# Where the high parts of the output projections' rows begin: from 160 to 288 modulo 512 bytes

## The chip, the cores and the metric

The kernel runs on one core of a Trainium2 chip. The metric is the device time of one execution in microseconds. Matmuls run on TensorE (PE), with weight loads shown as a row of their own (PEld); VectorE (DVE) and ScalarE (ACT) prepare operands; SyncE (SP) issues nearly all transfers.

## The reference

One layer of a transformer, 256 tokens of width 2048, all in float32. It is three blocks, each with an adaptive layer norm ahead and a gated residual with a second layer norm behind:

```python
h = _swiglu(_modulate(x, sh1, sc1), ffn1_w_in, ffn1_w_out)
x = _layernorm(ALPHA * x + 0.5 * (1 + g1) * h, ln1_g, ln1_b)
h = _token_mixer(_modulate(x, sh2, sc2), w_in, ..., w_out)
x = _layernorm(ALPHA * x + (1 + g2) * h, ln2_g, ln2_b)
h = _swiglu(_modulate(x, sh3, sc3), ffn2_w_in, ffn2_w_out)
x = _layernorm(ALPHA * x + 0.5 * (1 + g3) * h, ln3_g, ln3_b)
```

`_swiglu` is `(silu(gate) * up) @ w_out` with an inner width of 5632. The three products with `ffn1_w_out` (5632 x 2048), `w_out` (2048 x 2048) and `ffn2_w_out` (5632 x 2048) are the output projections of the title.

## The kernel before

Every float32 product is made of three products in the `fp32r` type. An operand is split in a high part (a cast on ACT, line 142) and a low part (what the cast lost, a subtraction on DVE, line 143), and `mm3` issues high x high (line 373), high x low (line 374) and low x high (line 375) into one accumulation. Three such matmuls are called a trio below.

In an output projection (`out_proj`) the rows, that is the activations, are the stationary operand (128 x 128, loaded on PEld), and the weights are the moving operand (128 x 512, streamed past them). For each k of 128 rows of the weights, each half `a` of the tokens and each block `b` of 512 columns there is one trio:

| line | moving operand | stationary operand |
|---|---|---|
| 373 | high part of weights (`hi`) | high part of rows (`hh`) |
| 374 | low part of weights (`lo`) | high part of rows (`hh`) |
| 375 | high part of weights (`hi`) | low part of rows (`hl`) |

The names in the trace are `o_f<-hi_f1o,hh` for the first feed-forward block (`f1o`), `f2o` for the second, and `o_mx<-hi_mxo,yhi` for the mixer, where the rows of the eight attention heads are `yhi`, `ylo`, and those of the other eight k are `yh`, `yl`, tiles of another pool that nothing here moves. In the feed-forward blocks `h_rows` splits the rows, two k at a time, into one of six buffers `hh` and one of six `hl`; the very first two k of each block go to two tiles of their own, laid out elsewhere, that the trace calls `h`.

Where a tile begins in a partition's memory follows from the order in which a pool's tiles are asked for. All weight buffers are whole multiples of 512 bytes long, and so are `hh`, `hl`, `yhi`, `ylo` and the activations `xhi`, `xlo` of the other products, so each kind has one place modulo 512:

| operand | modulo 512 before |
|---|---|
| `hi`, high parts of all weights | 288 |
| `lo`, low parts of all weights | 160 |
| `hh`, `hl`, `yhi`, `ylo` | 160 |
| `h` (both parts) | 448 |
| `xhi`, `xlo` | 480 |
| `yh`, `yl` | 8 places each, 128 to 392 |

`gap` asks for a tile that nothing uses, to move what comes after it:

```python
    for t in ("hhi", "hlo"):
        lnp.tile([P, 2, T], F32R, tag=t, bufs=6, name=f"{t}_place")
    gap(lnp, 320, "gap_h")
```

Ahead of the projections and between them, form A products (`s`, `gu_f`, `fs`, `fh`, `pr_f`) have the weights stationary and 256 tokens moving, and products such as `gf` have `xhi`, `xlo` stationary and 512 columns of weights moving, like an output projection with other rows.

Of the kernel before, what the change touches and what calls it, by code (L numbers as in the profile page):

```python
# [8 lines left out]
F32R = mybir.dt.float32r  # L9
# [6 lines left out]
P = 128  # L16
T = 256
# [6 lines left out]
NFH = 8  # L24
# [10 lines left out]
def layer_kernel(  # L35
# [13 lines left out]

    def gap(pool, nbytes, name):  # L50
        pool.tile([P, nbytes // 4], F32, tag=name, name=name)

    wp.tile([P, 4, 520], F32, tag="raw", bufs=3, name="raw_place")
    gap(wp, 320, "gap_hi")
    wp.tile([P, 1024], F32R, tag="hi", bufs=6, name="hi_place")
    wp.tile([P, 10], F32, tag="sums", bufs=4, name="sums_place")
# [179 lines left out]
    def need(n):  # L238
        while parts_done[0] < n and next(ada_left["g"], 0) != 0:
            owed[0] = 0  # L240
# [234 lines left out]
    def ln_params(g, b, tag):  # L475
        lg = lnp.tile([P, D], F32, tag="lg", name=f"lg_{tag}")
        lb = lnp.tile([P, D], F32, tag="lb", name=f"lb_{tag}")
        SP.dma_start(lg, g.to_broadcast([P, D]))
        SP.dma_start(lb, b.to_broadcast([P, D]))
        return lg, lb  # L480
# [308 lines left out]
    xp.release()  # L789
    lnp = tc.alloc_tile_pool(name="ln1", bufs=1, **right)  # L790
    lgb = ln_params(ln1_g, ln1_b, "1")
    for t in ("hhi", "hlo"):
        lnp.tile([P, 2, T], F32R, tag=t, bufs=6, name=f"{t}_place")
    gap(lnp, 320, "gap_h")
    need(1)
    W = w_in[0]

# [12 lines left out]
    def finish1(products, add_up, st):  # L810
        need(2)
        hp.release()
        ent["xp"] = tc.alloc_tile_pool(name="xp2", bufs=1)
        gap(ent["xp"], 544, "gap_x")
        ent["np"] = tc.alloc_tile_pool(name="np2", bufs=1)
        ent["f"] = (products, add_up, st)
# [358 lines left out]
    lnp = tc.alloc_tile_pool(name="ln2", bufs=1)  # L1175
# [5 lines left out]
            need(4)  # L1181

    gap(lnp, 224, "gap_y")
    yhi, ylo = (lnp.tile([P, NFH, T], F32R, name=f"y{i}") for i in ("hi", "lo"))


    def y_rows(k):
# [67 lines left out]
    for j in range(2, 10):  # L1255
# [8 lines left out]
        for f in range(2):  # L1264
            i = 2 * j + f
# [11 lines left out]
    for j in range(2, 10):  # L1277
# [7 lines left out]
        for f in range(2):  # L1285
            i = 2 * j + f
# [9 lines left out]
    xp.release()  # L1296
    lnp = tc.alloc_tile_pool(name="ln3", bufs=1, **right)
    lgb = ln_params(ln3_g, ln3_b, "3")
    for t in ("hhi", "hlo"):
        lnp.tile([P, 2, T], F32R, tag=t, bufs=6, name=f"{t}_place")  # L1300
    gap(lnp, 320, "gap_h")

    def finish3(products, add_up, st):
        to_out(products, add_up, st, lgb)
# [33 lines left out]
```

## Time and profile before

| | us |
|---|---|
| median of 3 runs | 1966.28 (1964.45 to 1966.31) |
| profiled execution | 1965.57 |
| its span, first to last instruction | 1963.8 |
| around the span | 1.8 |
| PE busy | 1896.5 |
| DVE busy | 1495.8 |
| first feed-forward output projection, in the span | 541.3 to 786.0 |
| mixer's output projection | 1109.4 to 1206.0 |
| second feed-forward output projection | 1709.1 to 1952.0 |

Mean granted clock of TensorE is 0.993. A matmul's duration in the trace runs from its start to its modelled end and overlaps the next one's; what a matmul costs in a stream without gaps is the distance from its start to the next start, called its pitch below.

### The profile page before, as it was taken

How to read it: one execution, taken by the hardware profiler on the slowest of the kernel's cores; microseconds unless marked ns; L12 is line 12 of the kernel's file. 1: busy time of each engine (PE TensorE's matmuls, PEld its weight loads, DVE VectorE, ACT ScalarE, POOL GpSimd, SP SyncE). 2: the span in 40 equal slices, each digit the busy share in tenths (PEclk: the TensorE clock that was granted, in tenths of full speed). 3: DMA queues.
4: the chain of work that ended last, by engine and by line, in shares of the span. 5: the costliest groups of instructions: out<-in, count | busy, mean ns of one | idle time of the engine just before them, and what ended most of it. 6: DMA issues, size and time to landing. Idle time of an engine off the chain costs nothing.

```text
span 1963.8 us, 32259 instructions
## 1 busy us (share of the span) xinstructions
PE 1896.5 (97%) x13057; PEld 1727.6 (88%) x13057; DVE 1495.8 (76%) x1878; ACT 961.1 (49%) x1396; POOL 6.3 (0%) x17
## 2 busy tenths in 40 slices
PE   3999999999999999899999998999999999999997
PEld 3999999999988888588999786899999999988885
DVE  7788889777788897678888688777766655555776
ACT  3644354443454554745755544555444444444553
POOL 0000000000000000000000000000000000000000
PEclk9999999999999999999999999999999999999999
DMA  9998978899898786489888784888777765655552
GB/s 331 342 315 278 314 253 289 290 305 326 281 343 303 268 303 208 140 292 319 270 300 278 273 285 151 285 292 274 241 248 249 261 216 190 236 193 193 193 193 86
DMA packets 301820, 510.89 MB, mean 260 GB/s; under 512 B 10818, under 2 KB 158690, under 8 KB 300648
## 3 DMA queue, kind: packets, MB, share of 16 engines
q1 hardware_dynamic: 300808, 505.70, 76.2%
q0 software_dynamic: 864, 3.15, 0.5%
q8 instruction: 102, 1.67, 0.4%
q14 instruction: 46, 0.38, 0.0%
HBM read 506.71 MB, written 2.10 MB: 259 GB/s over the span
## 4 chain that ended last, share of the span: by engine, by line
PE 83%; DVE 8%; DMA 5%; ACT 2%; issue 2%; SPq 0%; DVEq 0%; ACTq 0%
PE gu_f L374 8%; PE gu_f L375 8%; PE gu_f L373 8%; PE o_f L373 8%; PE o_f L375 8%; PE o_f L374 8%; PE s L373 3%; PE s L375 3%; PE s L374 3%; DMA raw_s<-in_ffn_w_in_dram 2%; DVE lo_s L143 2%; PE fs L375 1%; PE fs L374 1%; PE fs L373 1%; PE o_mx L373 1%
## 5 line engine op out<-in xcount | busy, mean ns | idle before, releaser
L157 DVE SCALAR_TENSOR_TENSOR acc<-ar,csil,acc 128x1024 f32<-128x1024 f32 x242 | 307.8, 1272 | 74.6 <-DMA ar<-in_w_ada_dram 72.9
L373 PE MATMUL s<-xhi_f,hi_s 128*128 128x256 f32 x768 | 215.0, 280 | 3.0 <-ACT hi_s L142 3.0
L375 PE MATMUL s<-xhi_f,lo_s 128*128 128x256 f32 x768 | 214.4, 280 | 1.9 <-DVE lo_s L143 1.9
L374 PE MATMUL s<-xlo_f,hi_s 128*128 128x256 f32 x768 | 214.2, 279 | 0.0
L375 PE MATMUL gu_f<-xhi_f,lo_f2i 128*128 128x256 f32 x768 | 212.0, 276 | 0.0
L373 PE MATMUL gu_f<-xhi_f,hi_f2i 128*128 128x256 f32 x768 | 212.0, 276 | 0.0
L374 PE MATMUL gu_f<-xlo_f,hi_f2i 128*128 128x256 f32 x768 | 212.0, 276 | 0.0
L143 DVE TENSOR_TENSOR lo_f2i<-raw_f2i,hi_f2i 128x1024 fp32r<-128x1024 f32 x96 | 117.6, 1225 | 91.4 <-ACT hi_f2i L142 91.4
L373 PE MATMUL gu_f<-xhi_f,hi_f1i 128*128 128x256 f32 x640 | 176.8, 276 | 0.0
L375 PE MATMUL gu_f<-xhi_f,lo_f1i 128*128 128x256 f32 x640 | 176.7, 276 | 0.0
L374 PE MATMUL gu_f<-xlo_f,hi_f1i 128*128 128x256 f32 x640 | 176.7, 276 | 0.0
L142 ACT CAST hi_f2i<-raw_f2i 128x1024 fp32r<-128x1024 f32 x96 | 100.8, 1050 | 135.4 <-PE gu_f L374 124.6
L373 PEld LDWEIGHTS s<-xhi_f,hi_s 128*128 128x128 f32 x768 | 146.2, 190 | 3.5 <-ACT hi_s L142 3.4
L142 ACT CAST hi_s<-raw_s 128x1024 fp32r<-128x1024 f32 x96 | 96.6, 1049 | 107.0 <-DMA raw_s<-in_ffn_w_in_dram 85.9
L375 PEld LDWEIGHTS s<-xhi_f,lo_s 128*128 128x128 f32 x768 | 145.9, 190 | 2.9 <-DVE lo_s L143 2.8
L374 PEld LDWEIGHTS s<-xlo_f,hi_s 128*128 128x128 f32 x768 | 146.4, 191 | 0.0
L374 PEld LDWEIGHTS gu_f<-xlo_f,hi_f2i 128*128 128x128 f32 x768 | 144.2, 188 | 0.2
L373 PEld LDWEIGHTS gu_f<-xhi_f,hi_f2i 128*128 128x128 f32 x768 | 144.2, 188 | 0.2
L375 PEld LDWEIGHTS gu_f<-xhi_f,lo_f2i 128*128 128x128 f32 x768 | 144.2, 188 | 0.0
L142 ACT CAST hh<-hT 128x512 fp32r<-128x512 f32 x130 | 80.0, 622 | 127.9 <-PE o_f L374 126.6
L143 DVE TENSOR_TENSOR lo_f2o<-raw_f2o,hi_f2o 128x1024 fp32r<-128x1024 f32 x88 | 107.7, 1224 | 44.9 <-ACT hi_f2o L142 44.8
L143 DVE TENSOR_TENSOR lo_s<-raw_s,hi_s 128x1024 fp32r<-128x1024 f32 x96 | 114.5, 1221 | 30.6 <-ACT hi_s L142 30.6
(452 smaller groups left out, 5385.2 us busy)
## 6 DMA issues: line engine op xcount, KB each, us to landing
ar<-in_w_ada_dram SPq DMA_DIRECT2D x288, 512.0 KB, 5.4
raw_s<-in_ffn_w_in_dram SPq DMA_DIRECT2D x48, 1024.0 KB, 6.1
raw_f2i<-in_ffn_w_in_dram SPq DMA_DIRECT2D x48, 1024.0 KB, 5.2
raw_f1o<-in_ffn_w_out_dram SPq DMA_DIRECT2D x44, 1024.0 KB, 7.4
raw_f2o<-in_ffn_w_out_dram SPq DMA_DIRECT2D x44, 1024.0 KB, 5.1
raw_f1i<-in_ffn_w_in_dram SPq DMA_DIRECT2D x40, 1024.0 KB, 7.7
raw_mxo<-in_w_out_dram SPq DMA_DIRECT2D x16, 1024.0 KB, 6.1
raw_fh<-in_ffn_w_in_dram SPq DMA_DIRECT2D x16, 1024.0 KB, 7.3
```

The costliest lines, as they stand in the source:

```text
L142: S.copy(hi, src)
L143: return V.tensor_tensor(out=lo, in0=src, in1=hi.bitcast(F32), op=ALU.subtract)
L157: V.scalar_tensor_tensor(out=acc, in0=raw, scalar=csil[:, k:k + 1], in1=acc, op0=ALU.mult, op1=ALU.add)
L373: PE.matmul(o, ah, bh, start=start, stop=False)
L374: PE.matmul(o, ah, bl, start=False, stop=False)
L375: PE.matmul(o, al, bh, start=False, stop=stop)
```

## The change

In the pool of the first and of the third layer norm the low parts of the rows are placed first (still 160 modulo 512), then 128 bytes that nothing uses, then the high parts (now 288), then 192 bytes. In the second, `ylo` comes first (160), then 128 bytes, then `yhi` (288). No other tile changes its place modulo 512; `hl` and `ylo` change their absolute place, in the same memory. The order of instructions on each of the five engines, their shapes and the waits they carry are the same in both programs, row for row.

```diff
-    for t in ("hhi", "hlo"):
+    for t in ("hlo", "hhi"):
         lnp.tile([P, 2, T], F32R, tag=t, bufs=6, name=f"{t}_place")
-    gap(lnp, 320, "gap_h")
+        gap(lnp, 128 if t == "hlo" else 192, f"gap_{t}")
...
     gap(lnp, 224, "gap_y")
-    yhi, ylo = (lnp.tile([P, NFH, T], F32R, name=f"y{i}") for i in ("hi", "lo"))
+    ylo = lnp.tile([P, NFH, T], F32R, name="ylo")
+    gap(lnp, 128, "gap_yhi")
+    yhi = lnp.tile([P, NFH, T], F32R, name="yhi")
...
-    for t in ("hhi", "hlo"):
+    for t in ("hlo", "hhi"):
         lnp.tile([P, 2, T], F32R, tag=t, bufs=6, name=f"{t}_place")
-    gap(lnp, 320, "gap_h")
+        gap(lnp, 128 if t == "hlo" else 192, f"gap_{t}")
```

## Rows read from the trace of the kernel before

**Rows 1.** The page's first part: busy time, share of span, instructions.

```profile
PE 1896.5 (97%) x13057; PEld 1727.6 (88%) x13057; DVE 1495.8 (76%) x1878; ACT 961.1 (49%) x1396; POOL 6.3 (0%) x17
```

**Rows 2.** Windows over the output projections: each engine's busy us, clock, DMA.

```profile
core 0: us, PE busy (x) PEld busy (x) DVE busy (x) ACT busy (x) POOL busy (x), PEclk, DMA share, GB/s
541.30:786.00 244.70, 244.70 (x1070) 200.11 (x1068) 213.69 (x244) 127.12 (x166) 0.53 (x1) 1.00 0.81 284
1109.40:1206.00 96.60, 96.60 (x422) 78.32 (x421) 75.79 (x96) 39.50 (x63) 0.55 (x1) 0.98 0.75 260
1709.10:1952.00 242.90, 241.99 (x1058) 197.89 (x1056) 164.29 (x182) 123.75 (x159) 0.00 (x0) 1.00 0.54 183
```

**Rows 3.** PE and PEld in order of time, two trios of the first projection.

```profile
611.05 0.39 PE L373 MATMUL o_f<-hi_f1o,hh 128*128 128x512 f32 x1
611.05 0.19 PEld L374 LDWEIGHTS o_f<-lo_f1o,hh 128*128 128x128 f32 x1
...
611.28 0.39 PE L374 MATMUL o_f<-lo_f1o,hh 128*128 128x512 f32 x1
611.28 0.19 PEld L375 LDWEIGHTS o_f<-hi_f1o,hl 128*128 128x128 f32 x1
611.51 0.39 PE L375 MATMUL o_f<-hi_f1o,hl 128*128 128x512 f32 x1
611.51 0.19 PEld L373 LDWEIGHTS o_f<-hi_f1o,hh 128*128 128x128 f32 x1
```

**Rows 4.** Groups by line and shape, PE: count, busy us, mean ns, idle before.

```profile
L373 PE MATMUL o_f<-hi_f2o,hh 128*128 128x512 f32 x344 | 135.2, 393 | 0.0
L375 PE MATMUL o_f<-hi_f2o,hl 128*128 128x512 f32 x344 | 134.5, 391 | 0.0
L374 PE MATMUL o_f<-lo_f2o,hh 128*128 128x512 f32 x344 | 133.5, 388 | 0.0
L373 PE MATMUL o_mx<-hi_mxo,yhi 128*128 128x512 f32 x64 | 26.3, 411 | 0.0
L375 PE MATMUL o_mx<-hi_mxo,yl 128*128 128x512 f32 x64 | 25.2, 394 | 0.0
L373 PE MATMUL o_f<-hi_f2o,h 128*128 128x512 f32 x8 | 3.2, 396 | 0.0
L375 PE MATMUL o_f<-hi_f2o,h 128*128 128x512 f32 x8 | 3.2, 396 | 0.0
L374 PE MATMUL o_f<-lo_f2o,h 128*128 128x512 f32 x8 | 3.2, 394 | 0.0
...
L373 PE MATMUL gu_f<-xhi_f,hi_f2i 128*128 128x256 f32 x768 | 212.0, 276 | 0.0
```

**Rows 5.** PE in order of time: first and last hh matmul, second projection.

```profile
1714.69 0.39 PE L373 MATMUL o_f<-hi_f2o,hh 128*128 128x512 f32 x1
...
1950.69 0.40 PE L375 MATMUL o_f<-hi_f2o,hl 128*128 128x512 f32 x1
```

**Rows 6.** PE in order of time: the first projection's start, first h, first hh.

```profile
541.27 0.40 PE L373 MATMUL o_f<-hi_f1o,h 128*128 128x512 f32 x1
...
546.86 0.39 PE L373 MATMUL o_f<-hi_f1o,hh 128*128 128x512 f32 x1
```

**Rows 7.** PE in order of time: gf, 69 matmuls from first to last row.

```profile
1341.49 0.40 PE L373 MATMUL gf<-hi_gu,xhi_f 128*128 128x512 f32 x1
...
1357.38 0.39 PE L373 MATMUL gf<-hi_gu,xhi_f 128*128 128x512 f32 x1
```

**Rows 8.** Matmuls with tile hh, second projection: durations ns min/median/max.

```profile
L373 PE MATMUL o_f<-hi_f2o,hh x344: 390/393/393, 1714.7 to 1950.2; 128*128 128x512 f32 x172
L374 PE MATMUL o_f<-lo_f2o,hh x344: 388/388/396, 1714.9 to 1950.5; 128*128 128x512 f32 x172
L142 ACT CAST hh<-hT x65: 614/622/637, 1710.5 to 1934.4; 128x512 fp32r<-128x512 f32 x65
```

## The prediction

> **What bounds the kernel now.** I read the page's busy times first: PE is busy for 97% of the span, DVE for 76% [rows 1]. That share alone says little about one stage, so I next took windows over the three output projections, the only stages where the moved tiles are read. In the first feed-forward projection PE is busy for 244.70 of 244.70 us, in the mixer's for 96.60 of 96.60, in the second for 241.99 of a window that ends just after its last matmul; the granted clock is 1.00, 0.98 and 1.00 [rows 2], the higher of the two levels, so nothing here turns on the clock. Idle time ahead of the matmuls is 0.0 in each group [rows 4]. So these stages are as long as their matmuls make them, and the number that matters is the pitch: from one matmul's start to the next.
>
> The order of time shows who runs beside whom. The weight load of the next matmul starts within 0.01 us of the matmul ahead of it, takes 0.19 us, and is over before that matmul's pitch is [rows 3]. So loads are hidden whole; what can differ is how fast a matmul streams while a load reads beside it. In the second projection the first and the last matmul with `hh` or `hl` start 236.00 us apart, with 344 trios, hence 1031 steps, between them [rows 4, 5]: 228.9 ns a step, 686.7 ns a trio.
>
> The three lines of a trio are not equal. Durations are 393, 388 and 391 ns for lines 373, 374 and 375 [rows 4], 390.7 on the mean; the pitch is 161.8 less, so I take off that constant and get pitches of about 231, 226 and 229 ns. The shape, the type and the count are the same; what differs is the address of what streams and of what is loaded meanwhile:
>
> - 373 streams `hi` (288) while `hh` for 374 is loaded (160): 231 ns
> - 374 streams `lo` (160) while `hl` for 375 is loaded (160): 226 ns
> - 375 streams `hi` (288) while `hh` for the next 373 is loaded (160): 229 ns
>
> The one with equal places is the shortest. That other rows have other pitches is shown by the same weights beside other tiles. With `h` (448) the first 24 matmuls of the first projection take from 541.27 to 546.86, that is 232.9 ns each, 698.8 a trio [rows 6]. With `xhi`, `xlo` (480) `gf` takes from 1341.49 to 1357.38 for 69, that is 230.3 each, 690.9 a trio [rows 7]. So the place of the stationary operand is worth at least 12.1 ns a trio between 160 and 448.
>
> Here a rule of the Trainium skill speaks against the change. The page "TensorE: Matmul & The Clock Gate", in "Step-by-step: what each phase is for", says that PE has two independent read ports, one for the moving and one for the stationary operand, and that loading the next weights takes no read bandwidth from the running matmul. By it no place of a stationary operand would cost anything and the time would stay at 1965.6 us. This trace does not agree: 686.7, 690.9 and 698.8 ns a trio for three places of the rows.
>
> **The change part by part.** It adds, removes and moves no instruction and no wait, so there is no new stall to place; only addresses differ. What can change is counted from the groups: 344 trios in each feed-forward projection (the f1o groups have the counts of f2o's) and 64 in the mixer's rows `yhi`, `ylo` [rows 4], 752 trios. The 16 trios on `h` and the 64 on `yh`, `yl` keep their places. So one nanosecond a trio is 0.752 us of the kernel.
>
> After the change all three pairs have equal places: 288 beside 288, 160 beside 160, 288 beside 288. What is unknown is the pitch of a matmul that streams from 288 beside a load from 288; the trace has no such row. Bounds from the nearest rows:
>
> - Below: 373 and 375 take the pitch of 374, which has equal places already. By durations that is 5 and 3 ns less, 8 ns a trio, 752 x 8 = 6.0 us gained.
> - Above: all as slow as beside `h`. 698.8 - 686.7 = 12.1 ns a trio, 9.1 us lost.
> - Between: as beside `xhi`, `xlo`. 690.9 - 686.7 = 4.2 ns a trio, 3.2 us lost.
>
> Which to take? The pair alone does not set the pitch: 373 and 375 stream from the same place beside loads from the same tile kind, and yet differ by 2 ns, every time (393 and 391). And 374 is not always short: its durations reach from 388 to 396 [rows 8], and where line 375 in the mixer meets `yl` at eight places the mean is 394 [rows 4]. So a matmul's pitch carries something over from the one ahead of it; a short 374 stands behind a long 373. If that is so, three short ones in a row are not to be had by making the three pairs alike: what 373 saves, 374 pays. I therefore take a trio between what it is now and `gf`'s, 688.8 ns, the middle of the two, nearer to the low end than to the high one because the trio's middle product keeps both of its places: 2.1 ns x 752 = 1.6 us lost. Both ends stay for the range.
>
> The other users of the moved tiles are hidden. ACT's cast into `hh` takes 622 ns, 65 times in a stage [rows 8], 40 us of 243, and ACT is busy for 123.75 us of that window [rows 2]; were each cast a tenth slower, 4 us more would lie in ACT's idle half. DVE is at 213.69 of 244.70 us and the DMA engines at 0.81 in the tightest of these stages [rows 2]. A gain of 8 ns x 344 trios = 2.75 us there would lift both to 88% and 0.82, so the weights still come in time and PE keeps the gain; a loss has nothing to hide behind, since PE has no idle time in these stages and the second layer norms wait for its last product.
>
> **The sum.** Profiled execution 1965.57 us = span 1963.8 + 1.8 around it; the median of the runs is 1966.28, 0.7 above. Likeliest: 1965.6 + 1.6 = 1967.2 us. A change under 0.2%, 3.9 us or 5.2 ns a trio, is about what a measurement of this kernel cannot tell from none.
>
> **The rivals.**
>
> 1. *Equal places are what makes 374 short, and the other two follow.* 752 trios at 8 ns less: 1965.6 - 6.0 = 1959.6 us, 0.3% faster. For it: the only equal pair is the shortest, with medians of 388 beside 393 over 344 trios [rows 8]. Against it: 373 and 375 differ though their pairs are alike, and of the three kinds of rows above none has a trio below today's 686.7. It decides from 5.2 ns a trio on.
>
> 2. *The new place is one of the bad ones.* A matmul that streams from 288 beside a load from 288 meets it from the first column on, at each of two places in the trio, and goes at the pitch beside `h`: 1965.6 + 9.1 = 1974.7 us, 0.5% slower. For it: of the three steady kinds of rows that the trace has, 160 is the best, and the other two cost 4.2 and 12.1 ns a trio more; a place picked blindly would fall between them. Against it: the pair 160 beside 160 is the shortest, and 288 beside 288 is the same but for a shift of 128 bytes. It decides from 692 ns a trio on, just above `gf`'s pitch.
>
> 3. *Nothing changes, since the place of the rows is not what slows the `h` and `gf` trios.* The `h` trios stand at the start of a stage, `gf` in another. 1965.6 us. For it: 686.7 and 690.9 differ by under 1%, and lines 373 and 375 differ at equal places. Against it: the `h` trios are as slow at the start of the second projection (396, 394 and 396 ns, 8 each, [rows 4]) as at that of the first [rows 6]. This is how it would go by the page of the Trainium skill named above.
>
> **How the numbers follow.** My forecast, a trio within 5.2 ns of today's, gets 0.46, with the third rival's 0.10 in it; its own range is 1962 to 1970. The first rival gets 0.25, the second, with everything above 692 ns a trio, 0.29. So faster by over 0.2%: 0.25; within 0.2%: 0.46; slower: 0.29. The range for 8 in 10 goes from the gain of the first rival, 1959.6, to the loss of the second, 1974.7, so to 1959.5 and 1975: neither tail can be left out, each holds over 2 in 10, and the bounds of the unknown pitch are these two.
>
> **What would show it.** In the profile after, the starts of the first and last `hh` matmul of the second projection lie 344 x trio apart: about 237 us by the forecast, 233 by the first rival, 240 by the second. By the first rival all three lines have 388 ns; by my forecast line 373 is shorter than 393 and line 374 or 375 longer than now; by the second all three are at 394 or more. The `h` and `gf` groups, the form A products (276 ns for `gu_f`, [rows 4]) and the loads of 0.19 us must stay as they are; if they move, something other than the place of `hh` is at work. The forecast is wrong if PE shows idle time ahead of o_f matmuls, since then a supplier, not the pitch, sets these stages; or if the trio leaves 682 to 692 ns.

## The result, and the profile after

| | median us | runs | ratio to before on the same chip, 95% interval |
|---|---|---|---|
| before | 1964.93 (1963.42 to 1966.31) | 5 | |
| after | 1975.96 (1972.93 to 1978.8) | 5 | 1.0043 [1.0025, 1.0061] |

In these runs the kernel is slower by 0.43%. The five runs of before lie within 2.9 us of each other; the 35 of the next comparison lie between 1960.48 and 1977.18, so five of a kind place a median only to some microseconds. The profiled execution of the changed kernel took 1978.69 us, with a span of 1977.0, 13.1 more than before. All rows of it have their line numbers one higher: 374, 375 and 376 are the three products of a trio.

Its page, first part (busy us, share of the span, instructions), to be held against [rows 1]:

```profile
PE 1906.7 (96%) x13057; PEld 1732.5 (88%) x13057; DVE 1497.7 (76%) x1878; ACT 961.9 (49%) x1396; POOL 6.3 (0%) x17
```

PE has 10.2 us more for the same 13057 matmuls; DVE and ACT have 1.9 and 0.8 more. The windows over the three output projections, with the columns of [rows 2]:

```profile
543.80:790.90 247.10, 247.01 (x1070) 200.40 (x1069) 214.81 (x244) 128.18 (x166) 0.53 (x1) 1.00 0.81 280
1119.40:1216.50 97.10, 95.69 (x422) 77.18 (x421) 77.35 (x103) 41.12 (x67) 0.55 (x1) 1.00 0.74 257
1719.90:1965.10 245.20, 244.25 (x1058) 198.17 (x1056) 164.35 (x182) 123.82 (x159) 0.00 (x0) 1.00 0.54 181
```

In the feed-forward projections PE is as full as before and the granted clock is 1.00, so they are still as long as their matmuls make them. The groups by line and shape (count, busy us, mean ns, idle before) tell which matmuls changed:

```profile
L374 PE MATMUL gu_f<-xhi_f,hi_f2i 128*128 128x256 f32 x768 | 212.0, 276 | 0.0
...
L375 PE MATMUL o_f<-lo_f2o,hh 128*128 128x512 f32 x344 | 136.1, 395 | 0.0
L374 PE MATMUL o_f<-hi_f2o,hh 128*128 128x512 f32 x344 | 134.9, 392 | 0.0
...
L376 PE MATMUL o_f<-hi_f2o,hl 128*128 128x512 f32 x344 | 134.7, 391 | 0.0
...
L374 PE MATMUL o_f<-hi_f2o,h 128*128 128x512 f32 x8 | 3.2, 396 | 0.0
```

Against [rows 4] the high x high product went from 393 to 392 ns, high x low from 388 to 395, low x high stayed at 391; `h` and `gu_f` are as they were. The product that grew by 7 ns is the one whose own two places did not change. Means hide what happens, so here is PE in order of time: two trios of the first projection (cut within the second), and the last `hl` matmul behind the first `hh` matmul of the second:

```profile
614.12 0.40 PE L374 MATMUL o_f<-hi_f1o,hh 128*128 128x512 f32 x1
614.35 0.40 PE L375 MATMUL o_f<-lo_f1o,hh 128*128 128x512 f32 x1
614.59 0.40 PE L376 MATMUL o_f<-hi_f1o,hl 128*128 128x512 f32 x1
614.82 0.39 PE L374 MATMUL o_f<-hi_f1o,hh 128*128 128x512 f32 x1
...
615.50 0.40 PE L374 MATMUL o_f<-hi_f1o,hh 128*128 128x512 f32 x1
...
1725.50 0.39 PE L374 MATMUL o_f<-hi_f2o,hh 128*128 128x512 f32 x1
...
1963.76 0.39 PE L376 MATMUL o_f<-hi_f2o,hl 128*128 128x512 f32 x1
```

One trio takes 0.70 us, the next 0.68, and so on in turn; before, a trio took 0.69, step by step 0.23 [rows 3, 5]. Nothing distinguishes the two but what ran ahead of them. From the first to the last row of the second projection are 238.27 us (the starts to the nanosecond; the rows, rounded, give 238.26) where it was 236.00 [rows 5]: over the same 1031 steps that is 231.1 ns a step and **693.3 ns a trio**, 6.6 more than 686.7.

So 752 x 6.6 = 5.0 us is what the trios can have cost, if the mixer's 64 changed alike (where they follow without a gap, theirs went from 686.8 to 694.3 ns on the mean). Stage by stage, the span's 13.1 us more are: 2.2 up to the first `gu_f` matmul, 0.4 in the first form A stage, 3.1 in the first projection (2.0 of it between the first and the last `hh` matmul, 1.1 behind), 4.4 from there to the mixer's projection, -0.6 in that, 1.3 up to the second form A stage, 0.0 in it, 2.3 in the second projection. Only the 2.0, the 2.3 and a part of the mixer's stand where tiles moved. The rest, some 8 us, had to be settled by runs.

A part of that rest can be read from the trace, and it is the clock. Here is one stretch of the stage up to `gu_f`, with the columns of [rows 2]:

```profile
249.00:256.50 7.50, 7.43 (x37) 7.43 (x38) 2.97 (x10) 4.22 (x9) 0.00 (x0) 0.54 0.48 162
```

PE is busy in it, but the granted clock is 0.54, so most of it ran at the lower level (1.2 GHz). PE had waited 2.07 us just before, in front of its matmul at 249.07. Up to the start of the last `o_f` matmul, 30.7 us of this execution have the lower level in the trace's clock record, against 20.5 in before. At half the clock 10.2 us more of that kind cost about 5.1 us if PE is busy throughout (an estimate from these two numbers). With the trios' 5.0 they make up the 10.2 us by which PE's busy time grew; the last 2.9 of the 13.1 us are idle time.

### The profile page after: what moved, and what is told of

The parts are those of the page before. It is cut to its first block, busy times and chain, and to the rows that moved or that the text cites. A ratio compares the mean times of both kernels' runs of the same rounds, so it can differ in the third digit from the quotient of the medians.

```text
span 1977.0 us, 32259 instructions
## 1 busy us (share of the span) xinstructions
PE 1906.7 (96%) x13057; PEld 1732.5 (88%) x13057; DVE 1497.7 (76%) x1878; ACT 961.9 (49%) x1396; POOL 6.3 (0%) x17
## 4 chain that ended last, share of the span: by engine, by line
PE 78%; DVE 9%; DMA 8%; ACT 3%; issue 2%; DVEq 0%; ACTq 0%; SPq 0%
PE o_f L375 8%; PE gu_f L374 8%; PE o_f L374 8%; PE gu_f L375 8%; PE gu_f L376 8%; PE o_f L376 8%; DMA raw_s<-in_ffn_w_in_dram 4%; DMA ar<-in_w_ada_dram 2%; DVE lo_s L144 2%; PE s L376 2%; PE s L375 2%; PE s L374 2%; DVE acc L158 2%; PE fs L375 1%; PE fs L374 1%
```

## The experiments

Theory A is that the pitch is all (4.8 to 5.0 us, 0.25%), and that the rest of the first difference is waits that vary from one execution to the next. Theory B is that the whole 11 us comes with the change. Each row below is one profiled execution, in us, read from PE in order of time: first to last `hh` or `hl` matmul of the first and of the second projection, the time up to the first `gu_f` matmul, from the first high x high `mo` matmul to the first of the mixer's projection, and the span.

| kernel | 1st projection | 2nd projection | up to `gu_f` | `mo` to `o_mx` | span |
|---|---|---|---|---|---|
| before | 239.00 | 236.00 | 320.61 | 292.24 | 1963.8 |
| after | 240.99 | 238.27 | 322.77 | 296.67 | 1977.0 |
| after again | 240.99 | 238.27 | 318.84 | 297.48 | 1971.5 |
| order of rows' parts alone | 239.00 | 236.00 | 322.94 | 294.03 | 1966.8 |
| last block alone | 239.00 | 238.27 | 316.54 | 298.66 | 1967.6 |
| low parts moved | 238.96 | 236.00 | 321.08 | 295.89 | 1966.7 |
| all four equal | 238.87 | 233.70 | 319.44 | 296.13 | 1969.6 |
| all four equal, a place skipped | 236.74 | 233.70 | 317.91 | 292.66 | 1957.0 |
| pieces at the old place | 239.00 | 236.00 | 318.75 | 294.88 | 1963.7 |

**The change once more**, the same kernel, no edit.

> The changed kernel once more, beside the kernel before on one chip. Theory A: all of the loss is the pitch of the 752 trios (693.3 instead of 686.9 ns, 4.8 us), and what the first comparison showed beyond that (11.0 us by the medians) came of waits that differ from one execution to the next: then the median is 4 to 6 us above before. Theory B: the change costs about 11 us every time, half of it outside the trios: then 9 to 13 us above, with the same extra waits in the stages ahead of the first output projection.

Measured: 1972.06 us beside 1969.13 of before, ratio 1.0012 [0.9994, 1.0029]. The medians differ by 2.9 us, less than either theory has. The interval reaches to 5.7 us, so it holds the 5.0 of A and not the 11 of B; it holds 1 as well, so that the change costs anything at all is shown by the stages and not by this comparison. The two projections are the same to 0.01 us in both executions. The stage up to `gu_f`, where nothing that moved is read in the first six rows of the table, spreads from 316.5 to 322.9 us over them, and from 318.8 to 322.8 for this one kernel. Theory B falls.

What the first profile had above the trios did not come back. Up to its last `o_f` matmul the lower clock stands for 20.5 us, as in before, and PE's busy time is 5.1 us above before's 1896.5, which is what 752 trios account for:

```profile
PE 1901.6 (96%) x13057; PEld 1728.8 (88%) x13057; DVE 1496.5 (76%) x1878; ACT 961.3 (49%) x1396; POOL 6.3 (0%) x17
```

The runs of before move with the clock too: of its 35 in this comparison, the four with a mean granted clock of 0.994 took 1962.8 to 1964.7 us, the five with 0.988 to 0.990 took 1970.8 to 1977.2.

**The order of the parts alone**: low parts first, no gap between, both at 160.

```diff
-    for t in ("hhi", "hlo"):
+    for t in ("hlo", "hhi"):
```

(the same for `yhi`, `ylo`)

> Low parts of the rows ahead of the high parts as in the change, but both at 160 modulo 512 as before: absolute places change, places modulo 512 do not. If the place modulo 512 sets the pitch: trio 686 to 688 ns, lines at 393, 388 and 391 ns, and a time within 2 us of before. If the absolute place matters (which memory the high parts lie in), the trio goes to about 693 ns and the time 5 us or more above before. If merely building the program anew with other places costs time in the waits ahead (theory B without the pitch), 5 to 6 us above before with the trio at 687.

Measured: 1966.88 us, ratio 0.999 [0.9972, 1.0007], trios as before (236.00 us in the table). Lying elsewhere in memory, at the same place modulo 512, changes nothing.

**The last block alone**: the change's first and last hunks differ only by the block; here the last one was made and the others not.

```diff
     lgb = ln_params(ln3_g, ln3_b, "3")
-    for t in ("hhi", "hlo"):
+    for t in ("hlo", "hhi"):
         lnp.tile([P, 2, T], F32R, tag=t, bufs=6, name=f"{t}_place")
-    gap(lnp, 320, "gap_h")
+        gap(lnp, 128 if t == "hlo" else 192, f"gap_{t}")
```

> The change in the pool of the third layer norm alone, so only the second feed-forward projection (344 trios, the last 255 us) has its high parts at 288. By the pitch: 344 x 6.4 ns = 2.2 us above before, the trio at 693 there and at 687 in the first projection. Nothing that moves in it is used ahead of 1700 us: if the stages before that are longer than before by several us again, those waits do not come from the places of the rows.

Measured: 1969.68 us, ratio 1.0008 [0.9989, 1.0027], where one projection's 2.3 us would be 1.0012; so small a difference is not shown by the times. The stage from `mo` to `o_mx` took 298.66 us, longer than in the changed kernel, though nothing that moved here is read before 1700 us: the places of the rows are not what lengthened that stage. Within one execution both kinds stand side by side, as the durations (ns min/median/max) of the matmuls with tile `hh` show:

```profile
L373 PE MATMUL o_f<-hi_f1o,hh x344: 390/393/393, 542.8 to 781.4; 128*128 128x512 f32 x172
...
L373 PE MATMUL o_f<-hi_f2o,hh x344: 387/388/397, 1716.2 to 1954.0; 128*128 128x512 f32 x172
```

**The low parts moved instead**: `hh` stays at 160, `hl` and `ylo` go to 288.

```diff
     for t in ("hhi", "hlo"):
         lnp.tile([P, 2, T], F32R, tag=t, bufs=6, name=f"{t}_place")
-    gap(lnp, 320, "gap_h")
+        gap(lnp, 128 if t == "hhi" else 192, f"gap_{t}")
...
-    yhi, ylo = (lnp.tile([P, NFH, T], F32R, name=f"y{i}") for i in ("hi", "lo"))
+    yhi = lnp.tile([P, NFH, T], F32R, name="yhi")
+    gap(lnp, 128, "gap_ylo")
+    ylo = lnp.tile([P, NFH, T], F32R, name="ylo")
```

> The mirror of the change: high parts of the rows stay at 160, low parts go to 288, so none of the three products streams from where the load beside it reads (288 beside 160, 160 beside 288, 288 beside 160). If unequal places make a product slow by themselves, all three lines are at 391 ns or more and the trio at 695 to 700, 6 to 10 us above before. If what counts is the whole trio and the state that one product leaves to the next, no line can be told ahead; the trio lies between 680 and 700, and lines 373 and 375 need not be alike.

Measured: 1968.02 us, ratio 0.9989 [0.9973, 1.0004]. The groups of the second projection:

```profile
L373 PE MATMUL o_f<-hi_f2o,hh 128*128 128x512 f32 x344 | 135.4, 394 | 0.0
L375 PE MATMUL o_f<-hi_f2o,hl 128*128 128x512 f32 x344 | 134.7, 392 | 0.0
L374 PE MATMUL o_f<-lo_f2o,hh 128*128 128x512 f32 x344 | 133.7, 389 | 0.0
```

No pair has equal places any more (low weights at 160 stream while `hl` at 288 is loaded), and the middle product is as short as it was: 225.9 ns from its start to the next on the mean, before and here. That equal places made it short is refuted.

**Other places in the layer.** In two kernels the six buffers of `hh` and of `hl` stood at six places each. From here on places are given modulo 256 bytes as (`hh`, `hl`), so the 288 of the change is 32.

```diff
+    place_rows([(0, 0), (32, 32), (64, 64), (96, 96), (128, 128), (192, 192)])
...
+    place_rows([(160, 32), (160, 0), (160, 64), (160, 96), (160, 128), (160, 224)])
```

> Six buffers of each kind of rows at six places (modulo 256 bytes). First projection: high and low part of a buffer both at 0, 32, 64, 96, 128, 192. Second projection: high parts at 160 in all six, low parts at 32, 0, 64, 96, 128, 224. Theory C (the place of the high part alone counts, and only the place of the weights' high parts, 32, is a bad one): second projection 686.9 ns a trio for each buffer, so its first to last hh 236 us; first projection 693 at the buffer at 32 and 686.9 at the five others, 688 on the mean. Theory D (every place of the high part has a pitch of its own): first projection between 680 and 700 by buffer, a buffer below 684 among them being worth -2 us and more if all rows stood there; second projection 686.9 throughout. Theory E (the low part counts as well, and the fourth experiment only met two like places): second projection differs by buffer by 3 ns or more.

The second kernel, with `(0, 160), (64, 160), ...` and `(32, 0), (32, 64), ...`:

> First projection: high parts at 0, 64, 96, 128, 192, 224 (modulo 256 bytes), low parts at 160 in all six buffers. Second projection: high parts at 32 as in the change, low parts at 0, 64, 96, 128, 192, 224. Theory C (only high parts at the weights' own place are bad): first projection 686.9 ns a trio in each buffer, second 693 in each. Theory D (each place of the high part has its own pitch): first projection from 680 to 700 by buffer, with the same order of places as in the first projection of the run beside it; second 693 in each. Theory E (low parts count): second projection differs by buffer by 3 ns or more, and the first projection's buffers differ from those of the run beside it at the same place of the high part.

Measured, one execution each, which tells nothing of so small a difference: 1974.33 and 1972.91 us beside 1974.37 of before. Mean distance from one trio's start to the next, over 52 to 60 trios for each buffer: with `hh` at 160, 686.4 ns where `hl` is at 32, and 692.2 to 695.1 at 0, 64, 96, 128 and 224; with `hh` at 32, 693.5 to 702.9; with both at one place, 694.2 to 700.5; with `hl` at 160 and `hh` at six other places, 694.3 to 700.0. No buffer is below before's 686.7 by more than 0.3. So C falls, the low part does count (E), and the experiment with the low parts moved met a place as good as before's.

**A map, with nothing else running.**

> Not the layer: only trios of the output projections' form (128x512 moving, 128x128 stationary, three a trio, eight PSUM tiles in turn) on fixed tiles, with nothing else running but the loads of these tiles; the output is zeros. 80 stretches of 48 trios, one for each combination of places modulo 256 bytes of weights' high and low parts and rows' high and low parts; the letters a to h in a tile's name are 0, 32, ... 224, and o_bfff is before (weights 32 and 160, rows 160 and 160), o_bfbf the change. Theory F (the places alone set the pitch, DVE, ACT and transfers have no part in it): o_bfff and o_bffb 686.9 ns a trio, o_bfbf 693.3 with long and short trios in turn, the other stretches of the 64 within 2 ns of the buffers of the two runs before (692 to 703), so that before's place is one of the two best. Theory G (it is the crossing of these reads with other engines' and transfers' accesses): all 64 stretches alike within 2 ns, and below 686. Theory H (what counts is the distance from the weights' places, not the place itself): the four shifted copies of before (o_cggg, o_dhhh, o_eaaa, o_fbbb) 686.9 each and those of the change (o_cgcg, o_dhdh, o_eaea, o_fbfb) 693.3 each; by absolute places they would range from 687 to 703.

```python
for hi, lo, hh, hl in RUNS:      # 80 combinations of places, 48 trios each
    ...
    PE.matmul(o[a * 2 + b], bh[:, s], ah[:, w], start=first, stop=False)
    PE.matmul(o[a * 2 + b], bh[:, s], al[:, w], start=False, stop=False)
    PE.matmul(o[a * 2 + b], bl[:, s], ah[:, w], start=False, stop=last)
```

First and last high x high matmul of five stretches, in order of time:

```profile
450.45 0.39 PE L62 MATMUL o_bfbf<-hi_b,hh_b 128*128 128x512 f32 x1
483.02 0.40 PE L62 MATMUL o_bfbf<-hi_b,hh_b 128*128 128x512 f32 x1
...
1519.55 0.39 PE L62 MATMUL o_bfff<-hi_b,hh_f 128*128 128x512 f32 x1
1551.83 0.39 PE L62 MATMUL o_bfff<-hi_b,hh_f 128*128 128x512 f32 x1
...
2153.38 0.40 PE L62 MATMUL o_cggg<-hi_c,hh_g 128*128 128x512 f32 x1
2185.66 0.39 PE L62 MATMUL o_cggg<-hi_c,hh_g 128*128 128x512 f32 x1
...
2186.35 0.40 PE L62 MATMUL o_cgcg<-hi_c,hh_c 128*128 128x512 f32 x1
2218.95 0.39 PE L62 MATMUL o_cgcg<-hi_c,hh_c 128*128 128x512 f32 x1
...
2485.45 0.39 PE L62 MATMUL o_bbbb<-hi_b,hh_b 128*128 128x512 f32 x1
2517.41 0.39 PE L62 MATMUL o_bbbb<-hi_b,hh_b 128*128 128x512 f32 x1
```

Over 47 trios each: `o_bfbf`, the change, 32.57 us, 693.0 ns; `o_bfff`, before, 32.28 us, 686.8; both shifted by 32 bytes, 693.6 and 686.8; all four parts at one place, 31.96 us, 680.0. So F holds for the kernel's two cases: without DVE, ACT or transfers the trios are what they are in the layer, even the turn of 705 and 681 ns. G falls. H holds for the two settings that were shifted: behind the first eight trios, all four shifted copies of before have 686.7 to within 0.1, all four of the change 693.6. It does not hold everywhere: `o_ffbb` is `o_bbff` shifted by 128 bytes, and they have 700.1 and 697.2, with turns of trio times that differ too; `o_bbff` had 697.2 again in the next map, behind other stretches. So either the absolute place counts in some settings, or the period is longer than 256 bytes there; no run decides. The mean distances in ns behind the first eight trios of a stretch, for weights at 32 and 160 (row: place of `hh`, column: of `hl`):

```
  hl:   0     32     64     96    128    160    192    224
  0  700.0  690.2  700.0  693.2  693.3  697.7  700.0  693.3
 32  693.3  700.0  702.2  693.3  693.3  693.0  693.3  700.0
 64  700.1  693.3  700.0  700.1  697.8  686.6  693.3  691.1
 96  693.3  700.0  693.3  693.3  700.0  693.4  700.0  699.9
128  700.3  693.2  703.4  706.6  693.3  696.7  700.0  696.6
160  693.4  686.7  693.3  693.3  694.7  686.7  686.7  686.7
192  697.5  700.0  700.0  700.1  696.8  700.0  700.0  700.0
224  700.0  693.4  693.3  700.0  686.7  693.4  693.6  691.1
```

Before's 686.7 is the floor of this table, and five other stretches share it. The layer's two other kinds of rows stand in it as well: `xhi`, `xlo` of `gf` (480, so 224 and 224) with 691.1 ns beside 690.9 in the layer, `h` (448, so 192 and 192) with 700.0 beside 698.8. That every stretch would be within 2 ns of the buffers of the two kernels before did not come true: 17 of 24 are, 7 differ by 2 to 9 ns. There a buffer serves 4 to 8 trios in a row, here 48; that what ran ahead counts for some trios is a likely reason, and was not tested by itself.

**A map with equal weights, and of form A.** `o_bbbb` at 680.0 is below anything in the table. Can the layer have it?

> Again only trios on fixed tiles, with zeros as output. 64 stretches of 48 trios in the output projections' form with both parts of the weights at 32 and the rows' parts at each of 8 x 8 places (o_bb, then two letters); then 128 stretches of 48 form A trios (weights stationary, 256 columns of activations moving), weights at 32 and 160 (u_bf) or 32 and 32 (u_bb), the activations' parts at each of 8 x 8 places. Theory J (four equal places are the best that there is, 680.0 in the run before, the floor of three pitches of 226.7): o_bbbb 680.0 again, and no other below it; each form A trio at best half of that, 340.0, which the layer's form A has already at u_bfhh; u_bbbb 340.0 too. Theory K (680.0 was met by chance of what ran before it): o_bbbb elsewhere, near 693. For a layer with all parts at 32 what counts is u_bb at the place of the activations, hh: if it is 340.0, moving the low parts of weights costs form A nothing; if it is 345, it costs some 4000 form A trios 20 us, more than the 5.0 us that 752 trios would gain.

Measured: `o_bbbb` 680.0 again, at another point of the program and behind other stretches, and nothing in its 64 below it (next 686.7), so K falls. Of J the part on form A falls: `u_bbbb`, which it had at 340.0, has 359.8. Two form A stretches, first and last high x high matmul:

```profile
3229.04 0.28 PE L74 MATMUL u_bfhh<-hh_h,hi_b 128*128 128x256 f32 x1
...
3245.06 0.28 PE L74 MATMUL u_bfhh<-hh_h,hi_b 128*128 128x256 f32 x1
...
4318.45 0.28 PE L74 MATMUL u_bbhh<-hh_h,hi_b 128*128 128x256 f32 x1
...
4335.06 0.28 PE L74 MATMUL u_bbhh<-hh_h,hi_b 128*128 128x256 f32 x1
```

With the weights at one place form A takes 16.61 us for 47 trios, 353.4 ns, against 340.0 (median) with the layer's places. `u_bfhh` is the only one of 128 stretches below 349. Moving the weights' low parts for good would cost each form A trio 13 ns (there are 768 of `s`, 1408 of `gu_f`, 256 each of `fs`, `fh` and `pr_f` and 128 of `pr_m`, 3072 in all and not the 4000 of the expectation), some 40 us; with the activations moved as well to the best of the 64 places, 349.9, still some 30. So the places must be equal in the output projections alone.

**All four equal in the output projections.** The high parts of weights lie in one tile with 128 bytes to spare, and only `out_proj` takes them 128 bytes further ahead, at 160, where `lo`, `hh` and `hl` already are. Such a matmul's tile is called `hi_all`; the lines are 380 to 382.

```diff
-    gap(wp, 320, "gap_hi")
-    wp.tile([P, 1024], F32R, tag="hi", bufs=6, name="hi_place")
+    gap(wp, 192, "gap_hi")
+    hi_all = wp.tile([P, 32 + 6 * 1024], F32R, name="hi_all")
+    hi_n = [0]
+
+    def hi_tile(h, w, at=32):
+        at += hi_n[0] % 6 * 1024
+        hi_n[0] += 1
+        return hi_all[:, at:at + h * w].rearrange("p (h w) -> p h w", h=h)
...
-            hi = wp.tile([P, h, w], F32R, tag="hi", bufs=6, name=f"hi_{name}{q}")
+            hi = hi_tile(h, w, hi_at)
...
-                                         f"{tag}o{col}_{u}"):
+                                         f"{tag}o{col}_{u}", 0):
...
```

(the loads of `gu` take their pieces from `hi_all` too, at the old place)

> The kernel before, with the rows where they were (160 modulo 512), and the high parts of the output projections' weights, and of these alone, 128 bytes ahead of their place, so at 160 as well: high and low parts of weights and rows all begin at one place there (o_ffff, the same distances as o_bbbb in the maps). Form A and the products with 512 columns beside xhi, xlo keep the weights at 288 and 160. Theory J (distances alone): hh trios 680.0 instead of 686.7, all three lines near 226.7, first to last hh of the second projection 233.7 us instead of 236.0; the second projection's stage 2.3 us shorter (252.4), the first's 2.3 us shorter (273.5), and 752 x 6.7 = 5.0 us in all, 0.25%, a ratio of 0.9975; form A 340.0 and gf 691.1 as before. Theory L (in the layer, where DVE, ACT and transfers write to the same memory, the floor is not to be had, or the suppliers fall behind a faster PE): trios above 684 or idle time ahead of o_f, a ratio of 0.999 to 1.001.

Measured: 1970.83 us, ratio 1.0015 [0.9994, 1.0036]. The second projection took 233.70 us, as J has it; the time did not follow, and the first projection took 238.87 where J has 2.3 us less than 239.00. The waits of PE (us in total, times, longest) from the first projection on name what L had:

```profile
PE o_f L380 <- ACT hi_all L149: 2.1, 2, 1.1
...
PE o_f L381 <- DVE lo_f1o L150: 0.9, 2, 0.5
```

and in order of time the entry of the second projection is

```profile
1715.36 0.28 PE L382 MATMUL gu_f<-xhi_f,lo_f2i 128*128 128x256 f32 x1
1716.70 0.50 PE L380 MATMUL o_f<-hi_all,h 128*128 128x512 f32 x1 [1.07 <-ACT hi_all L149]
```

The first moved piece overlaps by 128 bytes the piece ahead of it, the last that form A reads; its cast waits for those matmuls. These waits are 3.0 us; J's 5.0 did not show at all, and what else took the rest is open.

**A place skipped at the entry**, and the control.

```diff
+        hi_n[0] += 1
```

(at the start of `out_proj`)

> The run before with one edit: at the start of each output projection one of the six places of the weights' high parts is passed over. There the first moved part overlapped by 128 bytes the part that the last form A matmuls still read, so its cast had to wait for them. Theory M (that wait is what ate the gain of 680 ns trios at the entries): 339 to 1343 ns pitches at the entries gone, 1 to 2 us in all, and the kernel 4 to 5 us under before, a ratio of 0.9975. Theory N (the rest is eaten elsewhere: DVE, which splits the weights, is behind the faster PE in the first projection): trios 680.0, stalls ahead of o_f on lo_f1o remain, 1 to 3 us, and the ratio lies between 0.998 and 1.001.

> Control: the weights' high parts in six fixed pieces of one tile as in the run before, but at their old place (288) everywhere. If the pieces alone cost nothing: trios 686.7 as before, no stalls in the projections, a ratio of 1.000 (0.999 to 1.001). If the pieces cost something (waits at another tile's end): the same trios but a ratio of 1.002 or more; the difference of the two kernels of this call is then what the place alone gives, 5.0 us by 752 x 6.7 ns.

Measured: 1963.45 us, ratio **0.9978 [0.996, 0.9995]**; the control 1968.99, 0.9998 [0.9983, 1.0014]. The two medians differ by 5.5 us, where 752 x 6.7 ns is 5.0; the two feed-forward projections show 2.26 and 2.30 of it, the same kernels' stages in the table. With the place skipped, the groups and the window of the second projection:

```profile
L380 PE MATMUL o_f<-hi_all,hh 128*128 128x512 f32 x344 | 133.8, 389 | 0.0
L381 PE MATMUL o_f<-lo_f2o,hh 128*128 128x512 f32 x344 | 133.8, 389 | 0.0
L382 PE MATMUL o_f<-hi_all,hl 128*128 128x512 f32 x344 | 133.8, 389 | 0.0
```

```profile
1710.00:1945.00 235.00, 234.22 (x1034) 193.67 (x1032) 160.52 (x177) 119.25 (x151) 0.00 (x0) 1.00 0.55 184
```

All three lines are alike at 389 ns, and no wait for `hi_all` or `lo_f1o` is left: M holds for the waits, and those on DVE went with it. That they were all that ate the gain is not shown: the ratios of the two runs, 1.0015 and 0.9978, are some 7 us apart, the waits 3.0. This is the only kernel here whose interval lies below that of before as a whole; it was not run beside the changed one.

## Why the prediction came out as it did

**What bounds the kernel** was right: the projections are as long as their matmuls' pitches, loads stay hidden, no supplier comes late, and `h`, `gf` and `gu_f` did not change. The three pitches that it got by taking off a constant, 231, 226 and 229 ns, were near: from start to start they are 232.5, 225.9 and 228.4 on the mean of the second projection.

**The pitch carries something over** was right, and more than the text made of it: line 373's mean falls by 1 ns and line 374's rises by 7, though its places are the same; and two trios with the same six places take 705 and 681 ns in turn.

**The size is where it failed.** The step that took "a trio between what it is now and `gf`'s, 688.8 ns" was 4.5 ns short: the chip has 693.3, and 752 trios cost 5.0 us where 1.6 were set. The reason given, that the middle product keeps both of its places, had no weight: that product grew most, from 225.9 to 233.3 ns from start to start. With 693.3 the trio left the 682 to 692 of the forecast and passed the border at which the second rival decides, which had the sign (slower by over 0.2%) and too high a price, 9.1 us: its signs, 240 us and all three lines at 394 ns or more, did not come. By the pitch alone the time would have been 1965.6 + 5.0 = 1970.6, inside the range; the 1975.96 of the first five runs lies 1.0 above its end, the 1972.06 of the twelve later ones within it. That the first five lay so high was in part the luck of the draw: the profiled one of them, and no other can be looked into, had 10.2 us more at the lower clock than before, and the repeat of the kernel had none more. The text gave no share to waits and a clock that differ between executions; it looked at the clock in the three projections alone, and in the profiled ones a stage where nothing that moved is read spreads by 6.4 us.

**The first rival** (equal places make 374 short) fell with the change itself, three equal pairs at 693.3 ns, and again with the low parts moved. Yet its wish came true in another way: three products at the same short pitch are to be had, once all four parts, the weights' high and low too, begin at one place. It needed the low parts of the weights at the same place as the high ones, which the change leaves 128 bytes apart.

**The third rival** fell, and with it what the prediction took from the rule beside it. The page "TensorE: Matmul & The Clock Gate" of the Trainium skill, in "Step-by-step: what each phase is for", has the load of the next weights take no read bandwidth from the running matmul. No run here agrees with the consequence, that the place of a stationary operand costs nothing: the same shapes with nothing else running take 680.0 to 706.7 ns a trio by the operands' places alone. Whether it is the load that takes read bandwidth no run tells.

**Left open**: why the places matter. The runs show that a shift of all four parts changes nothing in two settings and 2.9 ns in a third; they do not show why, and they give no rule from which the table could be worked out.

## What to carry to other kernels

In a stage where PE is never idle, measure the distance from start to start, and treat the places of all operands that are read together, modulo 256 bytes here, as one setting: a change of one part alone can move the pitch of its neighbours. Such a map takes one short kernel of bare matmuls, and it told the pitch of before, of the change and of the four equal places in the layer to 0.3 ns, but not that of buffers that change every 4 to 8 trios (up to 9 ns off); each form of product has its own best places, so a place that is shared by two forms is a compromise that only separate places undo. A difference of 0.25% is read from the stage (236.00, 238.27, 233.70 us, the same to 0.01 in each of two to four executions) long before the whole time shows it. Before a rest is put down to a change, look at the granted clock of the stages around it.

## What had not been expected of the hardware

- The mean trio lies within 0.5 ns of 680.0, 686.7, 693.3, 700.0 or 706.7 ns, steps of 6.67 ns, in 65 of the 80 stretches of the first map; the mean pitch of a single product of a trio goes from 224 to 238 ns.
- A fixed pattern of addresses can run with a period of two trios (705 and 681 ns) for a whole stage, in the layer and in the map alike.
- All four operand parts at one place gave the lowest pitch of 128 combinations in this form, 226.7 ns a product, while form A with its two weight parts at one place had none below 349 a trio, and 340.0 with them 128 bytes apart and both parts of the activations at 224.
- A wait of about 2 us stood ahead of a stretch in which PE was busy at a granted clock of 0.54 (249.0 to 256.5 us), so an execution can lose more by such a wait than the wait itself.
